# Streaming 512 instead of 256 weight columns per matmul in the projections with stationary activations

## The chip, the core and the metric

One core of a Trainium2 chip runs the whole kernel. The metric is the time on the device in microseconds, from the first to the last instruction and what the runtime has around them. Each run is one launch. In the profile TensorE's work has two rows: PE, the matmuls, and PEld, the loads of the stationary operand. VectorE is DVE, ScalarE is ACT, GpSimd is POOL, and SyncE, which issues the weight DMAs, is SP.

## The reference

An encoder trunk of two layers on 256 tokens of width 1024, in float32. Every sub-layer is pre-norm (root mean square) and residual:

```
x = x + 0.5 * swiglu(norm(x))     # up and gate 1024 -> 2816 each, down 2816 -> 1024
x = x + mixer(norm(x))
x = x + 0.5 * swiglu(norm(x))
```

Layer 0's mixer is a gated linear attention with 4 heads, in both directions: q and k of 512 columns, v and an output gate g of 1024 columns, a low-rank gate for the log decay, then a norm by head, times silu(g), and an output projection 1024 -> 1024. Layer 1's mixer is differential attention with 8 heads: q, k and v of 1024 columns each, q and k normalized over 64 columns, two softmaxes per head with a relative-position bias, p1 - lambda * p2 times v, a norm by head, and an output projection.

## The kernel before

**Precision.** A product in float32 is made of three passes in float32r, a format that TensorE takes in one pass. Every weight piece and every activation is split into a high and a low part, and the kernel adds high x high, high x low and low x high. ScalarE makes the high part of weights (a copy), VectorE the low part (a subtraction), both at line 157 of the kernel before.

**Weights.** `weight_plan` lists all weights in the order of use, in pieces of 1024 rows x 256 columns (1 MB). `prefetch` issues one DMA per piece on SP's queue, up to five pieces ahead, into 3 staging buffers. `parts` splits a piece in operations of 128 x 1024 elements, up to three pieces ahead, into 5 buffers of split weights. `next_weights` hands out the next piece and starts both for later ones. `state["hold"]` keeps splits back around the end of a sub-layer, so that the norm's operations aren't queued behind them, and `release` lets them go.

**Two forms of projection.** In the feed-forward networks, in q and k of the gated attention and in the output projections the weights are stationary and the activations are streamed: `mm3` (lines 181 and 182) streams the high and low parts of all 256 tokens, 512 columns, against the high weights and then 256 columns against the low ones; `mm1` (lines 174 to 176) makes three matmuls of 256 columns. In the projections whose result must lie with tokens on the partitions the activations are stationary, 128 tokens at a time, and the weights are streamed: `project_tok` (lines 196 to 198), for v and g of the gated attention and q, k and v of the differential one, and `down_out` (lines 388 to 390), the last down projection, which writes the kernel's output. Each of these matmuls streams the 256 columns of a piece. A column group of 256 columns takes one accumulator bank, with its two halves of 128 tokens side by side.

**Accumulators.** Pool `psA` has six banks and serves the projections, scores and attention products; `psB` has two, for transposes and small sums.

**Order.** Each mixer has an order written out by hand. In it "h" is half a column group: one half of the tokens (24 matmuls) where activations are stationary. The other steps lie between the halves. For the differential mixer: b, statistics and scaling of q and k of a pair of heads (`qk_stats`); n, their transposes (`qk_norm`); s, scores and softmax of a head; f, transposed probabilities (`flip`); a, the product with v (`attend`); o, the norm and the transposed result (`normalize`). `qk_half` holds the raw q or k of a pair of heads in its bank until b has scaled it. The output projection (`out_proj`) adds up its first two column groups in parts, with the last pairs' steps between the parts. A planner then places the instructions: each engine has one queue, worked off in order, and the planner fills it in the written order, but puts an instruction that by its own estimate isn't ready behind others that are, and a tile waits until a buffer of its pool is free.

Of the kernel before, what the change touches and what calls it, by code (L numbers as in the profile page):

```python
# [18 lines left out]
P = 128  # L19
T = 256  # L20
# [9 lines left out]
CW = 256  # L30

# [20 lines left out]
DIFF_COLS = "q0 k0 q1 k1 v0 q2 k2 v1 q3 k3 v2 v3"  # L52


def weight_plan(w):
    """The weights in the order of use: [rows, columns] pieces of at most 1024 x 256, slices of rows, columns, copies."""
    plan = []

    def cols(a, start, width=CW, times=1):
        plan.append((a[:, start : start + width], KD, width, times))  # L60

    def ffn(i, j):
        gu, down = w["ffn_w_gu"][i, j], w["ffn_w_down"][i, j]
        for c in range(FF // CW):
            cols(gu, c * CW)
            cols(gu, FF + c * CW)
        for dc in range(D // CW):
            for k0 in range(0, NFB, KD):
                n = min(KD, NFB - k0)
                plan.append((down[k0 * P : (k0 + n) * P, dc * CW : (dc + 1) * CW], n, CW, 1))  # L70

    ffn(0, 0)
    gla = w["gla_w_in"][0]
    # four times side by side, to have the ranks on four groups of partitions
    cols(gla, gla.shape[1] - 32, 32, 4)
    for kind, c in GLA_COLS.split():
        cols(gla, {"q": 0, "k": 512, "v": 1024, "g": 2048}[kind] + int(c) * CW)
# [4 lines left out]
    for kind, c in DIFF_COLS.split():  # L82
        cols(w["diff_w_in"][0], "qkv".index(kind) * D + int(c) * CW)
# [7 lines left out]
def trunk(ctx: ExitStack, tc: tile.TileContext, ins, out):  # L91
# [19 lines left out]
    def prefetch(n):  # L111
        while state["dma"] < min(len(plan), n + LOOK_DMA + 1):
            i = state["dma"]
            src, nk, width, _ = plan[i]
            t = stage.tile([P, KD, CW], F32, tag="stage", name=f"stage{i}")
            step = nk if i > 1 else 2
            for k0 in range(0, nk, step):
                ks = slice(k0, k0 + step)
                nc.sync.dma_start(t[:, ks, :width], src.rearrange("(k p) n -> p k n", p=P)[:, ks])
# [3 lines left out]
    def parts():  # L123
        """The parts of the next weights to split."""
# [3 lines left out]
        w = split[i] = wpool.tile([P, KD, 2, CW], FR, tag="w", name=f"w{i}")  # L128
        state["split"] += 1
        step = 2 if i < 2 else 4  # L130
        for k0 in range(0, nk, step):
            ks = slice(k0, min(k0 + step, nk))
            whole, wh, wl = t[:, ks, :width], w[:, ks, 0, : times * width], w[:, ks, 1, : times * width]
# [17 lines left out]
    def issue(ops, after):  # L151
        """Each operation behind those of `after` that run on its engine."""
# [6 lines left out]
    def release(*after):  # L159
        """The parts held back, behind `after`."""  # L160
# [11 lines left out]
    def mm1(ps, w, ms, act, k, first, last):  # L172
        """ps += wh.xh + wh.xl + wl.xh for one 128-deep slice."""
# [4 lines left out]
    def mm3(ps, w, ms, act, k, first, last, wk=None):  # L178
        """ps[:, 0:256] += wh.xh + wl.xh, ps[:, 256:512] += wh.xl for one 128-deep slice."""
# [11 lines left out]
    def project_tok(w, act, name, ps=None, halves=(0, 1)):  # L191
        ps = psA.tile([P, 2, CW], F32, tag="A", name=name) if ps is None else ps
        for t in halves:
            ts_ = slice(t * P, (t + 1) * P)
            for k in range(KD):
                mm(ps[:, t, :], lhsT=act[:, k, 0, ts_], rhs=w[:, k, 0, :], start=k == 0, stop=False)  # L196
# [773 lines left out]
```

## Time and profile before

| | |
|---|---|
| three runs | 1000.81, 1001.91, 1004.33 us (median 1001.91) |
| profiled execution, span (the profile lists no other time for it) | 1000.1 us |
| TensorE matmuls | 6524, busy 994.5 us (99%) |
| TensorE weight loads | 6524, busy 906.6 us (91%) |
| VectorE, ScalarE | busy 748.0 us (75%), 567.7 us (57%) |
| HBM traffic | 178.95 MB, 179 GB/s on average |

The profile's first part has each engine's busy time. Matmuls are pipelined: a matmul's shown duration overlaps the next one's, so that the time between the starts of two tells what one costs in a row of them. In time the kernel is: feed-forward (0 to 195 us), gated attention with its output projection (195 to 320), two feed-forward networks (to 690), differential mixer (to 807), and the last feed-forward network, whose down projection runs from 932 us to the end.

### The profile page before, as it was taken

Reading aid. Unit: us, or ns where it says so; the run is one execution under the profiler, and the core shown is the slowest. Engines: PE = TensorE matmul, PEld = TensorE weight load, DVE = VectorE, ACT = ScalarE, POOL = GpSimd, SP = SyncE. Lnnn points to the kernel's source line nnn. Section 1 sums busy time; section 2 is a strip of 40 time slices with the busy share of each in tenths; the row PEclk is TensorE's granted clock in tenths of the full one; section 3 lists DMA queues with packets and bytes.
Section 4 is the critical chain, followed back from the end, with each engine's and each line's share of the span. In section 5 each row is a group of like instructions: output and inputs, shape, how many; then the busy total and the mean of one; then the engine's idle time right before and its main releaser. Section 6 shows DMA issues by size and latency. Waiting matters only on the chain.

```text
span 1000.1 us, 16172 instructions
## 1 busy us (share of the span) xinstructions
PE 994.5 (99%) x6524; PEld 906.6 (91%) x6524; DVE 748.0 (75%) x1284; ACT 567.7 (57%) x962; POOL 2.0 (0%) x10
## 2 busy tenths in 40 slices
PE   9999999999999999999999999999999999999998
PEld 8888888999999888888888888889999998888998
DVE  6998756499877987774679787656989699767640
ACT  7666535397756755643456555435576577555430
POOL 0000000000000000000000000000000000000000
PEclk9999999999999999999999999999999999999999
DMA  9676544574322775545557555375655268555440
GB/s 295 221 263 209 190 158 135 194 226 154 127 85 85 256 248 178 190 159 187 167 176 248 195 184 178 128 240 171 194 149 169 65 200 274 178 171 193 158 132 22
DMA packets 176968, 178.95 MB, mean 179 GB/s; under 512 B 4419, under 2 KB 176222, under 8 KB 176894
## 3 DMA queue, kind: packets, MB, share of 16 engines
q1 hardware_dynamic: 176606, 177.68, 54.3%
q8 instruction: 51, 0.84, 0.3%
q10 hardware_dynamic: 256, 0.21, 0.1%
q14 instruction: 23, 0.19, 0.1%
q0 software_dynamic: 32, 0.02, 0.0%
HBM read 176.84 MB, written 1.06 MB: 178 GB/s over the span
## 4 chain that ended last, share of the span: by engine, by line
PE 98%; DVE 1%; DMA 0%; ACT 0%; issue 0%; ACTq 0%; POOLq 0%
PE ps_g L181 16%; PE ps_u L181 16%; PE ps_d L181 12%; PE ps_g L182 8%; PE ps_u L182 8%; PE ps_d L182 6%; PE ps_d L388 2%; PE ps_d L389 2%; PE ps_d L390 2%; PE ps_s L567 2%; PE ps_dqk L196 2%; PE ps_dqk L198 2%; PE ps_dqk L197 2%; PE ps_w L174 1%; PE ps_w L176 1%; PE ps_w L175 1%
## 5 line engine op out<-in xcount | busy, mean ns | idle before, releaser
L157 DVE TENSOR_TENSOR w<-stage,w 128x1024 fp32r<-128x1024 f32 x334 | 385.4, 1191 | 32.2 <-ACT w L157 31.9
L157 ACT ACTIVATE w<-stage 128x1024 fp32r<-128x1024 f32 x334 | 327.3, 1030 | 45.4 <-PE ps_d L390 17.0
L181 PE MATMUL ps_g<-x,w 128*128 128x512 f32 x704 | 249.3, 397 | 0.0
L181 PE MATMUL ps_u<-x,w 128*128 128x512 f32 x704 | 248.7, 395 | 0.0
L182 PE MATMUL ps_u<-x,w 128*128 128x256 f32 x704 | 197.5, 281 | 0.0
L182 PE MATMUL ps_g<-x,w 128*128 128x256 f32 x704 | 197.1, 281 | 0.0
L181 PE MATMUL ps_d<-a,w 128*128 128x512 f32 x528 | 183.2, 390 | 0.0
L181 PEld LDWEIGHTS ps_g<-x,w 128*128 128x128 f32 x704 | 132.0, 188 | 31.0 <-issue 0.9
L181 PEld LDWEIGHTS ps_u<-x,w 128*128 128x128 f32 x704 | 132.0, 188 | 30.7
L182 PE MATMUL ps_d<-a,w 128*128 128x256 f32 x528 | 149.0, 282 | 0.0
L182 PEld LDWEIGHTS ps_g<-x,w 128*128 128x128 f32 x704 | 133.4, 189 | 0.5
L182 PEld LDWEIGHTS ps_u<-x,w 128*128 128x128 f32 x704 | 133.1, 189 | 0.1
L181 PEld LDWEIGHTS ps_d<-a,w 128*128 128x128 f32 x528 | 99.1, 188 | 20.7
L182 PEld LDWEIGHTS ps_d<-a,w 128*128 128x128 f32 x528 | 99.9, 189 | 0.0
L276 ACT ACTIVATE x<-x,par 128x256 fp32r<-128x256 f32 x40 | 20.0, 507 | 117.5 <-DVE x L325 117.5
L205 ACT COPY half<-ps_u 128x256 f32<-128x256 f32 x88 | 32.7, 371 | 87.2 <-PE ps_u L182 85.4
L205 ACT COPY half<-ps_g 128x256 f32<-128x256 f32 x88 | 32.3, 370 | 83.5 <-PE ps_g L182 81.4
L206 DVE TENSOR_TENSOR up<-ps_u,half 128x256 f32<-128x256 f32 x88 | 36.9, 422 | 38.7 <-ACT half L205 38.6
L206 DVE TENSOR_TENSOR gate<-ps_g,half 128x256 f32<-128x256 f32 x88 | 36.8, 422 | 36.9 <-ACT half L205 36.9
L325 DVE SCALAR_TENSOR_TENSOR x<-ps_d,x 128x256 f32<-128x256 f32 x48 | 20.3, 424 | 57.9 <-PE ps_d L182 56.7
L388 PE MATMUL ps_d<-w,a 128*128 128x256 f32 x176 | 49.5, 281 | 0.0
L389 PE MATMUL ps_d<-w,a 128*128 128x256 f32 x176 | 49.5, 281 | 0.0
(232 smaller groups left out, 1560.6 us busy)
## 6 DMA issues: line engine op xcount, KB each, us to landing
stage<-in_ffn_w_gu_dram SPq DMA_DIRECT2D x86, 1024.0 KB, 5.1
stage<-in_ffn_w_down_dram SPq DMA_DIRECT2D x32, 1024.0 KB, 4.8
stage<-in_ffn_w_down_dram SPq DMA_DIRECT2D x16, 768.0 KB, 4.1
stage<-in_gla_w_in_dram SPq DMA_DIRECT2D x12, 1024.0 KB, 5.6
stage<-in_diff_w_in_dram SPq DMA_DIRECT2D x12, 1024.0 KB, 5.5
stage<-in_gla_w_out_dram SPq DMA_DIRECT2D x4, 1024.0 KB
stage<-in_diff_w_out_dram SPq DMA_DIRECT2D x4, 1024.0 KB, 4.9
stage<-in_ffn_w_gu_dram SPq DMA_DIRECT2D x8, 256.0 KB, 5.7
```

What stands on the lines that cost most here:

```text
L157: op()
L181: mm(ps, lhsT=w[:, wk, 0, ms], rhs=act[:, k, :, :], start=first, stop=False)
L182: mm(ps[:, 0:T], lhsT=w[:, wk, 1, ms], rhs=act[:, k, 0, :], start=False, stop=last)
L196: mm(ps[:, t, :], lhsT=act[:, k, 0, ts_], rhs=w[:, k, 0, :], start=k == 0, stop=False)
L197: mm(ps[:, t, :], lhsT=act[:, k, 0, ts_], rhs=w[:, k, 1, :], start=False, stop=False)
L198: mm(ps[:, t, :], lhsT=act[:, k, 1, ts_], rhs=w[:, k, 0, :], start=False, stop=k == KD - 1)
L205: nc.scalar.copy(h[:, b, :], ps[:, T:512])
L206: nc.vector.tensor_tensor(out=out_t[:, b, :], in0=ps[:, 0:T], in1=h[:, b, :], op=ALU.add)
L325: nc.vector.scalar_tensor_tensor(out=x[:, d, :], in0=ps[:, h * T : (h + 1) * T], scalar=coef, in1=x[:, d, :], op0=ALU.mult, op1=ALU.add,)
L388: mm(ps, lhsT=act[:, k0 + k, 0, ts_], rhs=w[:, k, 0, :], start=first, stop=False)
L389: mm(ps, lhsT=act[:, k0 + k, 0, ts_], rhs=w[:, k, 1, :], start=False, stop=False)
L390: mm(ps, lhsT=act[:, k0 + k, 1, ts_], rhs=w[:, k, 0, :], start=False, stop=last)
```

## The change

- Weights of the five projections with stationary activations come in pieces of 512 rows x 512 columns (still 1 MB); two pieces make a column group of 512 columns, the last down projection takes 6 pieces for each of two groups. The splits have two rows' slices of 512 columns, still 128 x 1024 elements.
- Each matmul streams 512 columns. A bank holds 128 tokens x 512 columns, so a column group takes two banks, one after the other.
- In the mixers a column group is done in four quarters (class `Wide`): tokens 0 to 127 with the upper 512 rows, then the lower ones, then tokens 128 to 255 likewise. "h" is now a quarter where activations are stationary (12 matmuls of 512 columns); there are 24 "h" in each mixer as before.
- In the differential mixer a group of q or k covers two pairs of heads: the groups come as q0 k0 q1 k1 v0 v1 instead of q0 k0 q1 k1 v0 q2 k2 v1 q3 k3 v2 v3. Squares, sums and scaling run on one half of the tokens and 256 columns at a time, so there are twice as many, half as long. The order is written anew. In the output projection the parts are 4, 2 and 2 slices instead of 3, 3 and 2, and the norm and transposes of pair 2 lie between them as well.
- The tiles of the first softmax have 3 buffers instead of 4; those of v are twice as large.
- In the last down projection each bank is added to x in two operations of 256 columns and stored with one DMA of 256 KB.

```diff
 ORDER = """
-h h h h h h b0 h h n0 b1 h h s00 s01 n1 h h h f0 h s10 a0 s11 h h f1 b2 n2 h o0 a1 s20 s21 h h h b3 h f2 h n3 o1 a2 s30 s31 h h o2 hold
+h h h h h h h h b0 h n0 b1 h s00 s01 n1 h h f0 h s10 s11 h h h b2 f1 h n2 b3 h s20 s21 h n3 h a0 f2 s30 s31 a1 h o0 h o1 h h a2 hold
 """
-GLA_COLS = "q0 k0 q1 k1 v1 v0 g0 g1 v2 v3 g2 g3"
+GLA_COLS = "q0 k0 q1 k1 v0 g0 v1 g1"
-DIFF_COLS = "q0 k0 q1 k1 v0 q2 k2 v1 q3 k3 v2 v3"
+DIFF_COLS = "q0 k0 q1 k1 v0 v1"
...
+    def wide(a, c, nk=KD):
+        for k0 in range(0, nk, WK):
+            n = min(WK, nk - k0)
+            plan.append((a[k0 * P : (k0 + n) * P, c * WW : (c + 1) * WW], n, WW, 1))
...
-        step = 2 if i < 2 else 4
+        step = 2 if i < 2 or width == WW else 4
...
+    def mm_tok(ps, w, act, t, k0, nk):
+        ts_ = slice(t * P, (t + 1) * P)
+        for wk in range(w.shape[1]):
+            k = k0 + wk
+            mm(ps, lhsT=act[:, k, 0, ts_], rhs=w[:, wk, 0, :], start=k == 0, stop=False)
+            mm(ps, lhsT=act[:, k, 0, ts_], rhs=w[:, wk, 1, :], start=False, stop=False)
+            mm(ps, lhsT=act[:, k, 1, ts_], rhs=w[:, wk, 0, :], start=False, stop=k == nk - 1)
+
+    class Wide:
+        def __init__(self, act, name, done):
+            self.act, self.name, self.done = act, name, done
+            self.w = []
+
+        def quarter(self, n):
+            t, kh = divmod(n, 2)
+            if t == 0:
+                self.w.append(next_weights())
+            if kh == 0:
+                self.ps = psA.tile([P, WW], F32, tag="A", name=f"{self.name}_{t}")
+            mm_tok(self.ps, self.w[kh], self.act, t, kh * WK, KD)
+            if kh == 1:
+                self.done(t, self.ps)
...
+        for c in range(D // WW):
+            banks = [psA.tile([P, WW], F32, tag="A", name=f"ps_d{c}_{t}") for t in range(2)]
+            for k0 in range(0, nk, WK):
+                w = next_weights()
+                for t, ps in enumerate(banks):
+                    mm_tok(ps, w, act, t, k0, nk)
...
+                    for b in range(2):
+                        hp = 2 * c + b
+                        if i == 0 and t == 0:
+                            tot[hp] = small.tile([P, 2, 2, 4], F32, tag="dtot", name=f"dtot{hp}")
+                        sq = d2.tile([P, CW], F32, tag="dsq", name="dsq", bufs=1)
+                        nc.scalar.activation(sq, pq[:, b * CW : (b + 1) * CW], AF.Square)
+                        nc.vector.tensor_reduce(out=tot[hp][:, i, t], in_=sq.rearrange("p (g d) -> p g d", d=64), axis=AX.X, op=ALU.add)
...
-            out_proj(o2, n2, [range(0, 3), range(3, 6), range(6, 8)], [lambda: flip(3), lambda: attend(3), lambda: release(*normalize(3))])
+            out_proj(o2, n2, [range(0, 4), range(4, 6), range(6, 8)], [lambda: (normalize(2), flip(3)), lambda: attend(3), lambda: release(*normalize(3))])
```

## Rows read from the trace of the kernel before

**Rows 1.** Page, busy time of each engine: us, share of the span, instructions.
```profile
span 1000.1 us, 16172 instructions
PE 994.5 (99%) x6524; PEld 906.6 (91%) x6524; DVE 748.0 (75%) x1284; ACT 567.7 (57%) x962; POOL 2.0 (0%) x10
```
**Rows 2.** Page, the chain of work that ended last, shares by engine.
```profile
PE 98%; DVE 1%; DMA 0%; ACT 0%; issue 0%; ACTq 0%; POOLq 0%
```
**Rows 3.** Windows: length, busy PE PEld DVE ACT POOL, clock, DMA share, GB/s.
```profile
206.00:295.00 89.00, 89.00 (x733) 88.12 (x732) 79.45 (x102) 66.00 (x122) 0.00 (x0) 1.00 0.48 154
693.00:795.00 102.00, 101.19 (x883) 99.08 (x883) 87.17 (x288) 67.31 (x161) 0.00 (x0) 1.00 0.49 154
```
**Rows 4.** Groups by line and shape, TensorE: count, busy us, mean ns, idle before.
```profile
L388 PE MATMUL ps_d<-w,a 128*128 128x256 f32 x176 | 49.5, 281 | 0.0
...
L196 PE MATMUL ps_dqk<-w,x 128*128 128x256 f32 x128 | 36.6, 286 | 0.0
...
L196 PE MATMUL ps_g<-w,x 128*128 128x256 f32 x64 | 18.8, 293 | 0.0
```
**Rows 5.** Order of time, TensorE, q and k projection: start us, duration; 11 starts.
```profile
711.74 0.28 PE L198 MATMUL ps_dqk<-w,x 128*128 128x256 f32 x1
...
712.94 0.28 PE L196 MATMUL ps_dqk<-w,x 128*128 128x256 f32 x1
```
**Rows 6.** Order of time, TensorE, last down projection; 16 starts.
```profile
994.84 0.28 PE L390 MATMUL ps_d<-w,a 128*128 128x256 f32 x1
...
996.61 0.28 PE L390 MATMUL ps_d<-w,a 128*128 128x256 f32 x1
```
**Rows 7.** Order of time, TensorE, two feed-forward networks; three pairs each.
```profile
599.70 0.39 PE L181 MATMUL ps_g<-x,w 128*128 128x512 f32 x1
...
600.74 0.39 PE L181 MATMUL ps_g<-x,w 128*128 128x512 f32 x1
...
349.73 0.40 PE L181 MATMUL ps_u<-x,w 128*128 128x512 f32 x1
...
350.79 0.40 PE L181 MATMUL ps_u<-x,w 128*128 128x512 f32 x1
```
**Rows 8.** Chain of waits, gate logits: start us, us, what.
```profile
202.41 0.92 PE ps_z L543 x4
```
**Rows 9.** Chain of waits, gated attention's products with v; eight such rows.
```profile
269.85 0.43 PE ps_av L635 x2
```
**Rows 10.** VectorE in order of time, then groups by line, VectorE and ScalarE.
```profile
706.68 0.36 DVE L792 TENSOR_SCALAR dtot<-dtot,evx 128x8 f32<-128x8 f32 x2
...
709.17 0.17 DVE L217 SCALAR_TENSOR_TENSOR dr_y<-dr_t,dr_y 128x16 f32<-128x16 f32 x1
...
L780 DVE TENSOR_REDUCE dtot<-dsq 128x8 f32<-128x512 f32 x8 | 5.5, 682 | 3.2 <-ACT dsq L779 3.2
...
L288 ACT ACTIVATE sq<-x 128x256 f32<-128x256 f32 x42 | 16.8, 404 | 0.2 <-DVE acc L289 0.2
...
L779 ACT ACTIVATE dsq<-ps_dqk 128x512 f32<-128x512 f32 x8 | 4.7, 591 | 6.5 <-PE ps_dqk L198 6.5
...
L157 DVE TENSOR_TENSOR w<-stage,w 128x1024 fp32r<-128x1024 f32 x334 | 385.4, 1191 | 32.2 <-ACT w L157 31.9
```
**Rows 11.** TensorE in order of time, tail of the differential mixer.
```profile
787.30 0.36 PE L174 MATMUL ps_w<-do,w 128*128 128x256 f32 x1
...
791.47 0.28 PE L176 MATMUL ps_w<-do,w 128*128 128x256 f32 x1
792.46 0.63 PE L891 MATMUL ps_doT<-cst,do 128*128 128x128 f32 x4 [0.71 <-DVE do L883]
```
**Rows 12.** The end, VectorE; then DMA issues with KB and median us to landing.
```profile
996.93 0.42 DVE L392 SCALAR_TENSOR_TENSOR xt<-ps_d,xt 128x256 f32<-128x256 f32 x1 [1.70 <-PE ps_d L390]
...
stage<-in_diff_w_in_dram SPq DMA_DIRECT2D x12, 1024.0 KB, 5.5
...
out_dram<-xt SPq DMA_DIRECT2D x8, 128.0 KB, 1.9
```

More of the change, by code (lines that the diff above doesn't have):

```diff
@@ L66, in ffn @@
             cols(gu, FF + c * CW)
+        if (i, j) == (1, 1):
+            for c in range(D // WW):
+                wide(down, c, NFB)
+            return
         for dc in range(D // CW):
@@ L127, in parts @@
         t = staged.pop(i)
-        w = split[i] = wpool.tile([P, KD, 2, CW], FR, tag="w", name=f"w{i}")
+        w = split[i] = wpool.tile([P, nk, 2, times * width], FR, tag="w", name=f"w{i}")
         state["split"] += 1
-        step = 2 if i < 2 else 4
+        step = 2 if i < 2 or width == WW else 4
         for k0 in range(0, nk, step):
             ks = slice(k0, min(k0 + step, nk))
-            whole, wh, wl = t[:, ks, :width], w[:, ks, 0, : times * width], w[:, ks, 1, : times * width]
+            whole, wh, wl = t[:, ks, :], w[:, ks, 0, :], w[:, ks, 1, :]
             if times > 1:
@@ L189, in project @@
         return banks
[L191 to L196, printed above, removed]
-                mm(ps[:, t, :], lhsT=act[:, k, 0, ts_], rhs=w[:, k, 1, :], start=False, stop=False)
-                mm(ps[:, t, :], lhsT=act[:, k, 1, ts_], rhs=w[:, k, 0, :], start=False, stop=k == KD - 1)
-        return ps
+    def mm_tok(ps, w, act, t, k0, nk):
[18 more added lines that the diff above has]
+                self.done(t, self.ps)
     def join(banks, out_t):
@@ L509, in project_half, with done @@
                 def project_half(kind, c, n):
+                    if kind in "vg":
+                        def done(t, ps):
+                            if kind not in tm:
+                                tm[kind] = gp.tile([P, 2, GH * DV], F32, tag=kind, name=f"{kind}_tm")
+                            nc.scalar.activation(tm[kind][:, t, c * WW : (c + 1) * WW], ps, AF.Copy, scale=norm.r[:, t : t + 1])
+                        if n == 0:
+                            half[kind, c] = Wide(norm.x2, f"ps_{kind}{c}", done)
+                        half[kind, c].quarter(n)
+                        return
                     if n == 0:
@@ L513, in project_half @@
                     w, ps = half[kind, c]
-                    if kind in "vg":
-                        project_tok(w, norm.x2, None, ps, (n,))
-                        if n == 1:
-                            if kind not in tm:
-                                tm[kind] = gp.tile([P, 2, GH * DV], F32, tag=kind, name=f"{kind}_tm")
-                            for t in range(2):
-                                nc.scalar.activation(tm[kind][:, t, c * CW : (c + 1) * CW], ps[:, t, :], AF.Copy, scale=norm.r[:, t : t + 1])
-                        return
                     for k in range(KD):
@@ L661, in raw_scores @@
                     nc.scalar.copy(sd[hp], scores(qk[:, 0, gs], qk[:, 1, gs], f"ps_s0_{hp}"))
-                halves = [partial(project_half, g[0], int(g[1]), n) for g in GLA_COLS.split() for n in range(2)]
+                halves = [partial(project_half, g[0], int(g[1]), n) for g in GLA_COLS.split() for n in range(2 if g[0] in "qk" else 4)]
                 head, tail = (o.split() for o in GLA_ORDER.split("|"))
@@ L902, in diff @@
             for kind, c in DIFF_COLS.split():
-                half_of = partial(v_half, int(c)) if kind == "v" else partial(qk_half, int(c), "qk".index(kind))
-                halves += [partial(half_of, t) for t in range(2)]
+                c = int(c)
+                group = Wide(norm.x2, f"ps_d{kind}{c}", v_done(c) if kind == "v" else qk_done(c, "qk".index(kind)))
+                halves += [partial(group.quarter, n) for n in range(4)]
             steps = {"b": qk_stats, "n": qk_norm, "s": softmax, "f": flip, "a": attend, "o": normalize}
```

79 lines of the change are left out of this document (33 added, 46 removed).

## The prediction

> **What bounds the kernel now.** I read the busy shares first, then the chain of waits, then the stages' windows, and last the single matmuls in order of time. The first two say one thing: TensorE is busy 994.5 of 1000.1 us, and 98% of the chain that ended last runs through it [rows 1, 2]. So a matmul that gets cheaper shortens the kernel directly, and everything on the other engines costs something only where it makes TensorE wait. The windows show where that could happen. In the gated linear attention (206 to 295 us) TensorE is busy without a gap and VectorE 79.45 of 89 us; in the differential mixer (693 to 795 us) TensorE has 0.8 us of gaps and VectorE is busy 87.17 of 102 us [rows 3]. So the first has a little room, and the second hardly any. The granted clock is 1.00 in both, the 2.4 GHz level.
>
> **What a matmul costs.** A matmul's shown duration (281 ns for 256 columns) overlaps the next one's, so it is no price; the step from one start to the next is. In the differential mixer's projections 10 steps take 712.94 - 711.74 = 1.20 us: 120 ns for each 256-column matmul [rows 5]. In the last down projection 15 steps take 996.61 - 994.84 = 1.77 us: 118 ns [rows 6]. 256 columns at one a cycle of 2.4 GHz are 106.7 ns, so each carries some 11 to 13 ns that don't depend on its doing more work, if that part is fixed. Whether it is fixed decides the case. The projections in the feed-forward networks run 512 and 256 columns in turn, and three such pairs take 1.04 us in one network and 1.06 us in another: 347 and 353 ns a pair [rows 7], where three 256-column steps would be 360. With 118 to 120 ns for the 256-column half, the 512-column one takes 227 to 235 ns. One place of the trace has 512-column matmuls in a row, and in just the new form (stationary activations, float32r weights streamed): the gate's logits, four in 0.92 us, 230 ns each [rows 8]. I take 230 ns, that nearest row; the ends are 227 and 236.
>
> **The sum, part by part.** *Mixers.* The old projections are three lines (196 to 198) with 128 matmuls each for q and k of the differential mixer and 64 each for its v and for v and g of the gated attention (one row of 64 stands for three) [rows 4]: 3 x (128 + 3 x 64) = 960. They become 480. Each pair of 2 x 120 = 240 ns becomes 230: 480 x 10 ns = 4.8 us gained (6.2 us at 227, 1.9 at 236). q and k of the gated attention, the output projections and the gate and up projections are not touched.
>
> *Last down projection.* Three lines with 176 matmuls each [rows 4] are 528, and become 264. 2 x 118 = 236 becomes 230: 264 x 6 ns = 1.6 us gained (2.4 at 227, nothing at 236). TensorE has no gap here and the other engines are mostly idle, so all of it is on the path.
>
> *The end.* The last bank now holds 512 columns, added in two pieces of 256: one more 0.42 us VectorE operation between the last matmul and the last store [rows 12], +0.4. That store is 256 KB instead of 128: by the rows for 128 KB (1.9 us) and for 1024 KB of weights (5.5 us) another 128 KB takes 3.6 x 128 / 896 = 0.5 us [rows 12]; nothing if 2 KB rows go faster than 1 KB ones. I take +0.4, together +0.8 (0.4 to 0.9).
>
> *VectorE and ScalarE in the differential mixer.* Squares, their sums and the scaling by the norm now run on 256 columns of one token half: 16 of each where there were 8 on 512. A VectorE operation on 256 columns from the accumulators takes 0.42 us [rows 12] against 0.68 on 512 [rows 10], so 16 x (2 x 0.42 - 0.68) / 2 for each of two kinds: 2 x 8 x 0.16 = 2.6 us more. ScalarE: 8 x (2 x 0.404 - 0.591) = 1.7 us more [rows 10], less what v's copies save. Splitting the weights costs what it did: 128x1024 a time, 1191 ns [rows 10], as many times. All this lies beside TensorE, whose projections cover it; with the cover gone it is at most 2.6 us.
>
> *The order in the differential mixer.* A column group is now four quarters (t0 upper rows, t0 lower, t1 upper, t1 lower), each 12 matmuls or 2.8 us, as long as an old half. But q of pairs 0 and 1 comes whole before k, so the statistics of pair 0 start behind quarter 8 and not behind half 4, and four of the six banks stay taken until both pairs are scaled. What TensorE can run meanwhile are quarters 9 to 12, in the last two banks: 4 x 2.8 = 11 us, and about 3.4 us of transposes and scores. VectorE must do in that time: two sums 0.8; the statistics of pair 0, 709.34 - 706.68 = 2.7 us to the end of the reciprocal root, and four scalings of 0.42, together 4.4 [rows 10]; the same for pair 1, 4.4; the normalized q and k, two operations of 0.7; one weight piece of two splits, 2.4; the four passes over the first scores, 1.4. That is 14.8 us, and 17.2 with a second weight piece, behind 0.8 us of squares: 15.6 to 18.0 against 14.4 of cover. So a gap of 1.2 to 3.6 us can open, less what the weights split ahead (three pieces) let VectorE put off. At the second pair of groups the cover is longer, since v's quarters give their banks back at once and eight of them follow. I take +1.5 (0 to 4), the old 0.8 us of gaps standing as they are.
>
> *The tail of that mixer.* The output projection's first part is now four slices long, its second two, so behind the last attention product 24 matmuls are left and not 36. Today 36 run from 787.3 to 791.5 us and TensorE then waits until 792.46 us for the scaled product [rows 11]; at (791.47 - 787.30) / 35 = 119 ns a step, 12 fewer make that wait 1.4 us longer. But the third column group's weights are split by then and one bank is free, so its matmuls can fill in. I take nothing (up to 1.4).
>
> *Weights.* Pieces are still 1 MB, in the same number. The first two quarters of a group each take a piece, the next two none: two pieces in 2.8 us, then 8.3 us without. Five buffers hold two in use and three ahead, so this costs nothing; a piece that came late would show as a wait of ScalarE for the stage.
>
> Sum for the profiled execution: 1000.1 - 4.8 - 1.6 + 0.8 + 1.5 = 996.0 us, 4.1 less. The three runs before are 1000.81 to 1004.33 us, median 1001.91, so 1.8 us above the span; the median after is forecast at 997.8 us.
>
> **A rule against this size.** Where a pass has 512 cycles (two-pass float32 on 256 columns, the attention's products with v), the step is 0.43 / 2 = 0.215 us, though each loads other weights [rows 9]: 213.3 ns of streaming and almost nothing besides. The Trainium skill says the same of any matmul (TensorE: Matmul & The Clock Gate, Back-to-back issue gap): warm, the gap is N / 2.4 plus about 2.5 ns, so 109 ns for 256 and 216 for 512 columns. For the 256-column float32r matmuls the trace doesn't agree (118 to 120), and by the rule taken whole the change would be worth 744 x 2.5 ns = 1.9 us.
>
> **Rivals.** (a) *The extra goes away at 512*: it is there because a load and a stream of 256 columns are about as long, and a longer stream hides the load. Then the new matmul takes the 215 ns of [rows 9]: 480 x 25 + 264 x 21 ns = 17.5 us gained, less 2.3: 1001.9 - 15.2 = 986.7 us. For it: those rows. Against it: the 512-column matmuls of [rows 7] and [rows 8], which also hide their loads and take 227 to 235. (b) *The extra grows with the columns*: two 120 ns make 240, or the 236 that the slower network's share suggests. Gain 0 to 1.9 us, against 2.3 of costs: 1002.3 us, no change that can be told. For it: 230 is nearly twice 118. Against it: 347 ns a pair instead of 360. (c) *The banks decide*, and the kernel gets slower. The place is the differential mixer behind quarter 8: four of six banks are held, VectorE (already busy 85% of that stage) gets 2.6 us more, and TensorE runs out of work that has a bank. At the upper count, 3.6 us there, as much again behind quarter 16, the 2.6 us uncovered, and 1.4 at the tail: 11.2 us, against 6.4 gained and 0.8 at the end: 1001.9 + 5.6 = 1007.5 us. It decides once the gaps pass 5.6 us. For it: 15.6 to 18.0 us of VectorE chain in 14.4 us. Against it: the weights are split three pieces ahead, and quarters not bound to a bank can be put forward. (d) *It isn't what it says*, for instance still 960 steps of 120 ns: the matmul count would show it; I give it no chance of its own, the edit being plain.
>
> **How the numbers follow.** Forecast 0.62, (a) 0.11, (b) 0.12, (c) 0.15. The forecast's own ends: with 227 ns and no gaps 1001.9 - 8.6 + 0.4 = 993.7; with 236 and 4 us of gaps and 1.4 at the tail 1001.9 - 1.9 + 0.9 + 5.4 = 1006.3, so its likely part is 994 to 1004. The range that should hold the time 8 times in 10 reaches part of the way to (a) and to (c): 990 to 1005. What a measurement of this kernel can tell from no change is 0.3%, 3.0 us: faster is below 998.9, slower above 1004.9. The forecast's cases lie below 998.9 about seven times in ten. Faster: 0.62 x 0.72 + 0.11 = 0.56; slower: 0.15 x 0.85 + 0.02 = 0.15; same the rest, 0.29.
>
> **What would show it.** Right: 744 fewer matmuls and as many fewer loads; 512-column steps of 227 to 236 ns in the mixers and in the last down projection; the gated attention shorter by about 2 us and still without a gap (192 pairs), the last down projection by about 1.6. Wrong, by step: a step near 215 ns means (a), near 240 (b). The order's cost is TensorE's idle time between quarters 8 and 13; over 5 us there, with VectorE's scaling or a score's accumulator as what ended it, means (c). From the last matmul to the end it should take 0.8 us more.

## The result, and the profile after

The changed kernel takes 1017.19 us (median of four runs, 1012.91 to 1018.23); the kernel before, on the same chip, 1002.15 (1000.81 to 1004.33). The ratio is 1.0142, 95% interval 1.0125 to 1.0159: slower by 1.4%, where 0.4% faster was forecast. The profiled execution is the fastest of the four: span 1011.1 us against 1000.1.

First the page of the kernel after, answering to [rows 1, 2]: span, busy time of each engine, and the chain that ended last.

```profile
span 1011.1 us, 14705 instructions
...
PE 994.3 (98%) x5780; PEld 868.8 (86%) x5780; DVE 750.5 (74%) x1298; ACT 567.6 (56%) x956; POOL 2.0 (0%) x10
...
PE 71%; DVE 3%; ACT 1%; issue 0%; DVEq 0%; ACTq 0%
```

There are 744 matmuls and 744 loads fewer, as the edit says. The chain's shares add up to 75% only, since it is followed back from the end to 235 us and no further. So 71% for TensorE beside the 98% of before shows no loss by itself: narrow_diff below, which loses nothing, has 75%. What can be read is that VectorE has 3% where it had 1%, and ScalarE 1% where it had 0%. The busy time hardly fell: a busy TensorE also counts stretches at the lower clock and single matmuls whose shown duration is longer than their step.

The matmuls themselves, TensorE in order of time, with VectorE's last operation (answering to [rows 5, 6, 12]):

```profile
697.74 0.39 PE L210 MATMUL ps_dq<-w,x 128*128 128x512 f32 x1
...
700.91 0.39 PE L212 MATMUL ps_dq<-w,x 128*128 128x512 f32 x1
...
1002.72 0.40 PE L210 MATMUL ps_d<-w,a 128*128 128x512 f32 x1
...
1006.68 0.40 PE L212 MATMUL ps_d<-w,a 128*128 128x512 f32 x1
1007.12 0.76 DVE L420 SCALAR_TENSOR_TENSOR xt<-ps_d,xt 128x256 f32<-128x256 f32 x2 [0.65 <-PE ps_d L212]
```

14 steps in 3.17 us are 226 ns, 17 steps in 3.96 us are 233 ns; 230 was assumed. So the time isn't lost in the matmuls. The windows show where it is: the stretches of [rows 3] (the mixer's stage is longer now), the whole differential mixer, and a piece of it. Columns as there: length, busy PE, PEld, DVE, ACT, POOL, clock, DMA share, GB/s.

```profile
206.00:295.00 89.00, 88.85 (x556) 79.67 (x555) 80.69 (x104) 66.89 (x117) 0.00 (x0) 1.00 0.46 155
693.00:807.00 114.00, 103.80 (x606) 87.17 (x605) 89.28 (x302) 65.50 (x163) 0.00 (x0) 0.99 0.43 137
...
689.74:819.50 129.76, 119.56 (x726) 102.21 (x725) 102.93 (x331) 76.84 (x184) 0.00 (x0) 0.99 0.44 139
...
724.20:727.60 3.40, 3.40 (x19) 3.18 (x20) 3.40 (x13) 0.26 (x1) 0.00 (x0) 0.50 0.10 10
```

The whole mixer in the kernel before:

```profile
689.89:807.21 117.32, 116.51 (x1014) 114.40 (x1014) 100.83 (x317) 77.12 (x180) 0.00 (x0) 1.00 0.49 154
```

The mixer grew from 117.32 to 129.76 us, by 12.44, and TensorE's idle time in it from 0.81 to 10.20 us. VectorE's work grew by 2.1 us only. For 3.4 us the granted clock was 0.50, the 1.2 GHz level. The stages, each from its first matmul to the next stage's first:

| us | before | after | difference |
|---|---|---|---|
| start and first feed-forward network | 195.23 | 196.28 | +1.05 |
| gated attention with output projection | 124.47 | 123.24 | -1.23 |
| two feed-forward networks | 370.13 | 370.22 | +0.09 |
| differential mixer with output projection | 117.32 | 129.76 | +12.44 |
| gate and up of the last network | 127.09 | 125.82 | -1.27 |
| last down projection | 62.36 | 61.36 | -1.00 |
| last matmul's start to the end | 3.51 | 4.44 | +0.93 |

The first, third and fifth rows hold no changed instruction. They move by as much between other runs below with the same instructions there (the two feed-forward networks take 368.1 or 370.2 us, the fifth row 125.0 to 127.1), so they are left out of the account.

TensorE's waits in the mixer of the kernel after (waiter, line, what was waited for: us in total, times, longest):

```profile
PE ps_sc L845 <- ACT qkn L835: 3.2, 2, 2.3
PE ps_sc L845 <- DVE qkx L820: 2.3, 2, 1.7
PE ps_doT L914 <- DVE do L906: 2.1, 4, 0.7
PE ps_sc L845 <- DVE mx L852: 1.0, 1, 1.0
PE ps_f L828 <- DVE qkx L820: 0.7, 2, 0.3
PE ps_sc L845 <- DVE qkn L836: 0.5, 1, 0.5
PE ps_sc L845 <- ACT dv_tm L886: 0.5, 1, 0.5
```

Scores (ps_sc) wait for normalized q and k (qkn) and, where VectorE's scaling (qkx) or a score pass (mx) is named, for an accumulator bank that it frees; so does the copy of v (dv_tm). Of these 10.3 us, 3.7 are waits of scores for qkn and 3.8 for banks. Before there was one such wait, the scaled product's 0.71 us at the tail [rows 11]. The same wait after:

```profile
806.17 0.66 PE L914 MATMUL ps_doT<-cst,do 128*128 128x128 f32 x4 [0.60 <-DVE do L906]
```

Now both engines at the first pair of heads, in order of time. TensorE:

```profile
712.02 0.39 PE L210 MATMUL ps_dq<-w,x 128*128 128x512 f32 x1
...
716.78 0.39 PE L210 MATMUL ps_dq<-w,x 128*128 128x512 f32 x1
717.51 0.30 PE L828 MATMUL ps_f<-cst,qkx 128*128 128x128 f32 x1 [0.34 <-DVE qkx L820]
...
719.91 0.38 PE L845 MATMUL ps_sc<-qkn 64*128 64x256 f32 x1 [0.87 <-ACT qkn L835]
720.80 0.85 PE L845 MATMUL ps_sc<-qkn 64*128 64x256 f32 x5 [0.52 <-DVE qkn L836]
722.61 0.98 PE L845 MATMUL ps_sc<-qkn 64*128 64x256 f32 x6 [0.95 <-DVE mx L852]
724.16 2.04 PE L845 MATMUL ps_sc<-qkn 64*128 64x256 f32 x12 [0.58 <-DVE qkx L820]
...
727.68 0.48 PE L210 MATMUL ps_dq<-w,x 128*128 128x512 f32 x1
```

and VectorE:

```profile
712.64 0.42 DVE L801 TENSOR_REDUCE dtot<-dsq 128x4 f32<-128x256 f32 x1 [1.91 <-ACT dsq L800]
...
715.81 1.22 DVE L171 TENSOR_TENSOR w<-stage,w 128x1024 fp32r<-128x1024 f32 x1
716.95 0.75 DVE L820 TENSOR_TENSOR qkx<-ps_dq,dr_y 128x256 f32<-128x256 f32 x2
717.61 0.75 DVE L820 TENSOR_TENSOR qkx<-ps_dk,dr_y 128x256 f32<-128x256 f32 x2
718.27 1.22 DVE L171 TENSOR_TENSOR w<-stage,w 128x1024 fp32r<-128x1024 f32 x1
719.41 0.68 DVE L833 TENSOR_TENSOR qkn<-ps_f,qkn 128x512 fp32r<-128x512 f32 x1
720.01 0.74 DVE L836 SCALAR_TENSOR_TENSOR qkn<-ps_f,gqk,qkn 128x512 fp32r<-128x512 f32 x1
...
722.56 1.22 DVE L171 TENSOR_TENSOR w<-stage,w 128x1024 fp32r<-128x1024 f32 x1
723.69 0.75 DVE L820 TENSOR_TENSOR qkx<-ps_dq,dr_y 128x256 f32<-128x256 f32 x2
724.36 0.74 DVE L820 TENSOR_TENSOR qkx<-ps_dk,dr_y 128x256 f32<-128x256 f32 x2
```

From quarter 8's end TensorE has two quarters to run (712.0 to 717.0 us). The next quarter, 11, whose weights are those of quarter 9, starts at 727.68: in TensorE's queue it stands behind the transposes and scores of heads 0 and 1, and these wait for VectorE's chain, which takes 12.46 us from the first sum (712.64) to the last scaling of pair 1 (725.10). Three weight splits of 1.22 us lie inside it. The same pattern comes back at pairs 2 and 3, at 748 to 770 us.

### The profile page after: what moved, and what is told of

It is laid out like the page before. It is cut to its first block, busy times and chain, and to the rows that moved or that the text cites. A ratio compares the mean times of both kernels' runs of the same rounds, so it can differ in the third digit from the quotient of the medians.

```text
span 1011.1 us, 14705 instructions
## 1 busy us (share of the span) xinstructions
PE 994.3 (98%) x5780; PEld 868.8 (86%) x5780; DVE 750.5 (74%) x1298; ACT 567.6 (56%) x956; POOL 2.0 (0%) x10
## 4 chain that ended last, share of the span: by engine, by line
PE 71%; DVE 3%; ACT 1%; issue 0%; DVEq 0%; ACTq 0%
PE ps_u L195 12%; PE ps_g L195 12%; PE ps_d L195 8%; PE ps_g L196 6%; PE ps_u L196 6%; PE ps_d L196 4%; PE ps_d L212 2%; PE ps_d L210 2%; PE ps_d L211 2%; PE ps_s L597 1%; PE ps_w L188 1%; PE ps_w L189 1%; PE ps_w L190 1%; ACT s L860 1%; PE ps_sc L845 1%; PE ps_dk L211 1%
## 5 line engine op out<-in xcount | busy, mean ns | idle before, releaser
L171 ACT ACTIVATE w<-stage 128x1024 fp32r<-128x1024 f32 x332 | 326.9, 1036 | 55.6 <-PE ps_d L212 15.3
L211 PE MATMUL ps_d<-w,a 128*128 128x512 f32 x88 | 34.8, 396 | 0.0
L212 PE MATMUL ps_d<-w,a 128*128 128x512 f32 x88 | 34.8, 395 | 0.0
```

Of the source, the lines that this page charges most:

```text
L171: op()
L211: mm(ps, lhsT=act[:, k, 0, ts_], rhs=w[:, wk, 1, :], start=False, stop=False)
L212: mm(ps, lhsT=act[:, k, 1, ts_], rhs=w[:, wk, 0, :], start=False, stop=k == nk - 1)
```

## The experiments

Below, *gaps* are what the steps from one matmul's start to the next exceed those of an unbroken row, where that is over 0.15 us; this includes some slow steps at the lower clock. *Idle* is stage less busy TensorE. Both are for the differential mixer, in the profiled execution. A ratio is taken to the kernel before as it ran beside that kernel on the same chip (medians 1002.15 to 1003.62 us).

| kernel | median us | ratio to before, 95% | mixer us | gaps | idle | us at 1.2 GHz in it |
|---|---|---|---|---|---|---|
| before | 1002.15 | | 117.32 | 1.3 | 0.8 | 0 |
| after | 1017.19 | 1.0142 (1.0125 to 1.0159) | 129.76 | 13.5 | 10.2 | 3.4 |
| narrow_diff | 1000.83 | 0.9978 (0.9967 to 0.9989) | 117.31 | 1.3 | 0.8 | 0 |
| two256 | 1023.96 | 1.0211 (1.0189 to 1.0232) | 136.42 | 15.2 | 10.8 | 13.7 |
| order_h | 1008.37 | 1.0051 (1.0034 to 1.0068) | 122.24 | 7.6 | 6.3 | 0 |
| pairs | 1001.77 | 0.9993 (0.9978 to 1.0007) | 117.81 | 4.5 | 2.7 | 0 |
| chain1 | 1013.45 | 1.0097 (1.0083 to 1.0111) | 128.58 | 11.2 | 5.6 | 10.2 |
| hold_split | 1006.11 | 1.0022 (1.0007 to 1.0037) | 122.06 | 7.1 | 4.7 | 0 |
| order_hold | 1008.26 | 1.0050 (1.0036 to 1.0064) | 124.93 | 9.6 | 5.9 | 3.4 |
| hold_tail | 1003.19 | 1.0001 (0.9989 to 1.0013) | 121.70 | 6.5 | 4.3 | 0 |
| narrow_end | 1001.14 | 0.9979 (0.9968 to 0.9990) | 117.34 | 1.3 | 0.8 | 0 |
| pairs2 | 1000.60 | 0.9978 (0.9965 to 0.9990) | 118.09 | 4.7 | 3.0 | 0 |
| pairs3 | 1001.35 | 0.9982 (0.9972 to 0.9992) | 119.34 | 5.9 | 3.6 | 0 |
| chain_long | 1004.47 | 1.0011 (1.0000 to 1.0023) | 120.87 | 4.4 | 3.3 | 0 |
| long_one | 1012.72 | 1.0099 (1.0069 to 1.0129) | 128.72 | 11.1 | 8.9 | 10.2 |
| long_all | 1018.52 | 1.0152 (1.0128 to 1.0176) | 136.10 | 15.3 | 11.4 | 13.7 |

**narrow_diff**: the old differential mixer, all else changed.

```diff
-DIFF_COLS = "q0 k0 q1 k1 v0 v1"
+DIFF_COLS = "q0 k0 q1 k1 v0 q2 k2 v1 q3 k3 v2 v3"
-        wide(w["diff_w_in"][0], ...)
+        cols(w["diff_w_in"][0], ...)
```

> The changed kernel with the differential mixer of before (256 columns a matmul, its old order and output-projection parts); the gated attention's v and g and the last down projection stay at 512. Theory 'the whole loss is in the differential mixer, the other two places gain what the shorter stream gives': 192 pairs x 9 ns + 264 x 5 ns = 3.0 us less than before, less 0.5 us at the end: 999.7 us, TensorE's gaps in that mixer as before, 1.3 us, clock 1.00. Rival 'the wide weight pieces themselves cost (weights arrive in twos, longer last store)': over 1003 us, with gaps outside the differential mixer.

The mixer is back at 117.31 us, and the kernel is 0.2% faster than before. So the whole loss is in the differential mixer, and the rest of the change is worth some 2 us.

**two256**: the new order and groups, but each 512-column matmul as two of 256.

```diff
-            mm_tok(self.ps, self.w[kh], self.act, t, kh * WK, KD)
+            for j in range(2):
+                mm_half(self.ps[:, kh * CW : (kh + 1) * CW], self.w[j], ...)
```

> The changed kernel with every 512-column matmul issued as two of 256 columns (a quarter is then one half of the columns over all eight slices, so that each accumulation closes before the next opens; four banks instead of two per group in the last down projection); order, pieces, banks of the mixers and small operations as changed. Theory 'the fixed part of a matmul is saved': 480 x 9 + 264 x 5 = 5.6 us more than the changed kernel where TensorE does not wait; in the differential mixer the longer quarters cover part of the gaps, so 3 to 6 us more in time. Rival 'a 512-column matmul costs what two of 256 do': the same time within 1 us.

Idle is 10.8 us here too. So it comes with the grouping and its order, not with the width of a matmul. The median is 6.8 us above the changed kernel's, more than the 3 to 6 expected; 13.7 us at 1.2 GHz instead of 3.4 are in the profiled mixer. What the width alone is worth shows where TensorE never waits: the last down projection takes 62.36 us here, as in the kernel before, against 61.36.

**order_h**: the changed kernel with one more quarter ahead of the first transposes and of the first scores.

```diff
-h h h h h h h h b0 h n0 b1 h s00 s01 n1 h h f0 h s10 s11 ...
+h h h h h h h h b0 h h n0 b1 h h s00 s01 n1 h h f0 s10 s11 ...
```

> The changed kernel with another written order in the differential mixer alone: both quarters of the next group stand ahead of the transposes and the next two ahead of the scores (h x8, b0 h h n0 b1 h h s00 s01 n1 h h f0 s10 s11 h h b2 f1 h h n2 b3 h h s20 s21 n3 a0 h h f2 s30 s31 a1 h o0 h o1 a2). Theory 'order': TensorE's queue is worked off in order and stands at scores whose inputs the statistics chain on VectorE has not made, with ready quarters queued behind them; with the quarters ahead the gaps around the first two and the fifth to eighth scores (9 of 13.5 us) fall to 2 or 3 us and the kernel takes 1005 us. Rival 'banks': all six banks are then held by raw q and k when the first scores come, they wait until both pairs are scaled, the gaps stay at 9 us or more and the time within 3 us of the changed kernel's.

TensorE's waits in its mixer:

```profile
PE ps_w L188 <- ACT do L916: 2.4, 1, 2.4
PE ps_sc L845 <- DVE qkx L820: 2.2, 1, 2.2
PE ps_doT L914 <- DVE do L906: 1.3, 2, 0.7
PE ps_sc L845 <- DVE mx L852: 0.3, 1, 0.3
```

Gaps fall by 5.9 us and the mixer by 7.5. No score waits for qkn any more. What stays at the scores is 2.2 us for a bank: with four quarters run ahead, all six banks are held until the scaling. So two more quarters ahead of the scores give back 7.5 of the 12.4 us. A wait for a bank is left, and another (2.4 us) at the output projection, ahead of which the order now has no quarter left. The median, 1008.37 us, stays above the 1005 expected.

**pairs**: 512 columns made of 256 of q and 256 of k of one pair of heads, v's first group 512 wide and the other two 256, in the old order. A pair's statistics then need one group only.

```diff
-DIFF_COLS = "q0 k0 q1 k1 v0 v1"
+DIFF_COLS = "p0 p1 w0 p2 p3 v2 v3"
+                plan.append(([rows[:, i * D + c * CW : i * D + (c + 1) * CW] for i in range(2)], WK, WW, 1))
```

> 512 columns a matmul, but a group of the differential mixer holds 256 columns of q and the same 256 of k, so that it serves one pair of heads as before: two banks held per pair, squares, sums and scaling on 512 columns in as many operations as before, and the old written order. v of the first two pairs is 512 wide, v of the last two stays at 256. Both theories, order and banks, expect the gaps back at before's 1.3 to 3 us and the gain of the stream kept: (192 + 192 + 48) x 9 + 264 x 5 = 5.2 us, less 0.5 at the end: 997.5 us. If instead the doubled width itself disturbs the mixer (bursts of weights), gaps over 5 us and 1003 us or more.

Gaps of 4.5 us, no wait at a score: with 512-column matmuls the mixer costs what it did. But both theories expected gaps of 1.3 to 3 us and 997.5 us, and both missed: what the stream saves (20 quarters instead of halves) goes into new gaps, at the transposes above all (1.3 us of waits, none before).

**chain1**: the changed kernel with one Newton step instead of three in the reciprocal root of q's and k's statistics.

```diff
-                r = rsqrt(tot[hp]..., [P, 16], "dr")...
+                r = rsqrt(tot[hp]..., [P, 16], "dr", 1)...
```

> The changed kernel with one Newton step instead of three in the reciprocal root of the statistics of q and k in the differential mixer; two of three steps are left out, six small VectorE operations for each pair of heads. Theory A (VectorE's chain of statistics, splits, scaling and norm sets TensorE's gaps in that mixer): the chain of each pair of heads gets about 1.2 us shorter, so the gaps fall from 13.5 to 10 to 11.5 us and the span from 1011.1 to about 1008.5. Rival B (the order in TensorE's queue alone, with gaps of fixed length): gaps 13 to 13.5 us, span 1011. Rival C (accumulator banks alone): no change either, since the same tiles are held by the same instructions in front.

Its TensorE at pair 0, the waits ahead of the first drop of the clock:

```profile
717.02 0.30 PE L828 MATMUL ps_f<-cst,qkx 128*128 128x128 f32 x1 [0.16 <-DVE qkx L820]
...
720.36 0.86 PE L845 MATMUL ps_sc<-qkn 64*128 64x256 f32 x5 [0.32 <-DVE qkn L836]
722.17 0.97 PE L845 MATMUL ps_sc<-qkn 64*128 64x256 f32 x6 [0.95 <-DVE mx L852]
```

Up to there the idle time is 1.43 us against 2.68 in the changed kernel, and VectorE's chain takes 11.20 us against 12.46: both are 1.25 us shorter. So the chain sets the wait, and rivals B and C, which let nothing change, fall. Over the whole mixer idle falls further (10.2 to 5.6 us), but part of that is TensorE working at the lower clock where it would have waited: the clock stood at 1.2 GHz for 10.2 us instead of 3.4, about 3 of the 11.2 us of gaps are 0.2 us steps at that clock, and the mixer is only 1.2 us shorter. The profiled span is 1012.0 us, where 1008.5 was expected; the medians differ by 3.7 us.

**hold_split**: the changed kernel with VectorE's weight splits issued behind the scores of heads 1 and 5.

```diff
+                elif step in ("b0", "b2"):
+                    state["hold"] = "low"
+                    qk_stats(int(step[1]))
+                elif step in ("s01", "s21"):
+                    release(softmax(int(step[1]), int(step[2])))
```

> The changed kernel with VectorE's weight splits held back from the statistics of pair 0 until the last score pass of head 1, and again from the statistics of pair 2 until that of head 5; as many splits, later. Theory A (the splits of 1.2 us each stand inside VectorE's chain): 2.4 to 4.8 us leave the chains, gaps fall from 13.5 to 9 to 10.5 us, median 1017 to about 1012. Rival B (order in TensorE's queue alone): gaps 13 to 13.5 us. Rival C (the splits are then late for the projections behind the scores): gaps unchanged in sum or larger, with weight parts named as what TensorE waits for.

Its VectorE in order of time, first sum to the last scaling of pair 1:

```profile
710.99 0.42 DVE L801 TENSOR_REDUCE dtot<-dsq 128x4 f32<-128x256 f32 x1 [1.80 <-ACT dsq L800]
...
714.28 0.75 DVE L820 TENSOR_TENSOR qkx<-ps_dq,dr_y 128x256 f32<-128x256 f32 x2
...
718.70 0.75 DVE L820 TENSOR_TENSOR qkx<-ps_dk,dr_y 128x256 f32<-128x256 f32 x2
```

719.45 - 710.99 = 8.46 us against 12.46: the splits are gone from it. Gaps fall by 6.4 us and the mixer by 7.7, more than expected, and no weight part is waited for. In the mixer this gives as much as order_h (122.06 and 122.24 us), and it takes no column, bank or matmul away. The waits for a bank go with it, but for 0.3 us. (The planner also puts pair 0's transposes five matmuls earlier and moves later scores and transposes; the same work stands ahead of the first scores.)

**order_hold**: both together.

```diff
+h h h h h h h h b0 h h n0 b1 h h s00 s01 n1 h h f0 s10 s11 ...
+                elif step in ("b0", "b2"):
+                    state["hold"] = "low"
...
```

> The changed kernel in the other written order (as in the run of the other order before), and the splits held back as well. Theory A: gaps in the mixer fall from 7.6 to 4 to 5.5 us, span 1002.6 to about 1000. Rival C (splits late): gaps 7.6 us or more, with weight parts as what is waited for. Rival D (the rest of the gaps are bank waits that no split touches): 7 to 7.6 us.

No sum of both: 124.93 us. TensorE now waits 2.5 us for qkn ahead of the transposed probabilities (ps_T) and 1.5 for a score pass, and the clock falls for 3.4 us. The planner puts TensorE's work in another order for it, so this run doesn't tell which of its rivals holds.

**hold_tail**: hold_split with the output projection's old parts.

```diff
-[range(0, 4), range(4, 6), range(6, 8)]
+[range(0, 3), range(3, 6), range(6, 8)]
```

> The changed kernel with the splits held back as before, and the output projection of the differential mixer in the old parts of 3, 3 and 2 slices instead of 4, 2 and 2, so that 36 and not 24 matmuls stand behind the last attention product. Theory (the new parts cost at the tail what was bounded at 1.4 us): of the gaps at the three scaled products behind 780 us (0.85, 0.16 and 0.73 us) some 1.0 us goes, the stage falls from 122.1 to 121.1 us. Rival (the wait for the last scaled product is there with either, as in the kernel before with 0.7 us, and the other parts only move it): stage 122 us.

0.36 us in the mixer; the waits for the scaled product stay (1.3 us, two). The rival holds: the parts don't set the tail. The new order also leaves two pairs' norms for the tail where the old one leaves one; that wasn't tried by itself. The ratio falls by 0.0021, more than 0.36 us explain; the two intervals overlap. The median is that of the kernel before, but the new groups still cost: the mixer takes 4.4 us more than before, and the 2 us that narrow_diff gains in the other places stand against it.

**narrow_end**: narrow_diff with two stores for the last bank, on two queues.

```diff
-                        nc.sync.dma_start(out[0, ts_, cs], xt[:, t, cs])
+                            (nc.sync if h else nc.scalar).dma_start(out[0, ts_, ho], xt[:, t, ho])
```

> The kernel with the old differential mixer and everything else changed, and with each 128 x 256 piece of the last bank stored by a DMA of its own, on two queues, right behind its addition. Theory (the wider bank's end costs 0.9 us through one more addition and a larger store): the end from the last matmul falls from 4.44 to 3.9 us, span 998.5 to 998.0, ratio to the kernel before 0.997. Rival (the store's fixed latency decides): end 4.4 us, span 998.5.

The end falls from 4.44 to 4.05 us, as the theory has it to 0.15 us; in the median nothing of it can be seen.

**pairs2, pairs3**: attempts at a version that beats both, from pairs with narrow_end's stores; pairs2 with n0 and n2 a quarter later, pairs3 with hold_split's hold.

```diff
-h h h h h h b0 h h n0 b1 h h s00 ... f1 b2 n2 h o0 ...
+h h h h h h b0 h h h n0 b1 h s00 ... b2 f1 h n2 o0 ...
```

> The kernel whose 512 columns are q and k of one pair of heads, with the transposes of pairs 0 and 1 put one quarter later and each 128 x 256 piece of the last bank stored on its own. Theory A (the 4.5 us of gaps of that kernel are waits for a chain that is a fraction of a quarter late): gaps 4.5 to 2.5 to 3.5 us, stage 117.8 to about 116.5, end 4.9 to 4.1 us, ratio to the kernel before about 0.997. Rival B (the gap goes to the next step in the queue): stage 117.5 to 118.5 us, ratio 0.999.

> The kernel whose 512 columns are q and k of one pair of heads, in its old order, with VectorE's splits held back from the statistics of pair 0 to the last score pass of head 1 and from those of pair 2 to that of head 5, and each 128 x 256 piece of the last bank stored on its own. Theory A (a split of 1.2 us stands inside VectorE's chain at the two transposes that wait): gaps 4.5 to 2.5 to 3.5 us, stage about 116.5 us, ratio 0.997. Rival B (there is cover here, and later splits make the projections behind the scores wait): gaps 4.5 us or more with weight parts as what is waited for, ratio 1.000.

In both the gaps don't fall (4.7 and 5.9 us), as rival B has it; its reason in pairs3, weight parts that come late, isn't among TensorE's waits. At 0.2% faster than before they are no better than narrow_diff. No version here passes that: narrow_diff, narrow_end, pairs2 and pairs3 lie within each other's intervals.

**chain_long, long_one, long_all**: narrow_diff, so old order and 256 columns, with VectorE's chain made longer by more Newton steps: 13 at pair 0, 25 at pair 0, 11 at every pair.

```diff
-r = rsqrt(tot[hp]..., [P, 16], "dr")
+r = rsqrt(tot[hp]..., [P, 16], "dr", 13 if hp == 0 else 3)
```

> The kernel with the old differential mixer and everything else changed, with 13 Newton steps instead of 3 in the reciprocal root of pair 0 alone: 30 small VectorE operations, about 0.2 us each with the way from one to the next, so the chain of pair 0 is 6 us longer; nothing else differs. Theory A (the old order has cover behind the statistics, the new one has not): less than the 6 us shows, gaps in the mixer 1.3 to between 2 and 6 us, all before the first scores. Theory C (the level of 1.2 GHz comes behind gaps): where they reach some 3 us, a stretch of 3.4 us or more at granted clock 0.5 follows in the records, and costs half its length. Rival D (the level comes with the new order's mix of scores and transposes, not with gaps): granted clock 1.00 in the mixer whatever the gaps.

> The kernel with the old differential mixer and everything else changed, with 25 Newton steps instead of 3 in the reciprocal root of pair 0 alone. Ten steps more gave 5.2 us more of VectorE and 3.1 us more of gaps, so 22 more give 11.5 us of VectorE and gaps of 4.4 + 6.3 = about 10.5 us in the mixer, one of them some 8 us long; the stage is then about 127 us. Theory C (the level of 1.2 GHz follows gaps): granted clock 0.5 for one or two stretches of 3.4 us or more right behind the long gap, and run clocks of 0.993 to 0.998. Rival D (it comes with the new order's mix of scores and transposes): granted clock 1.00 in the mixer, run clocks 0.998 to 1.000.

> The same kernel with 11 Newton steps instead of 3 for every pair of heads: some 4.2 us more of VectorE for each of four pairs, 17 us in all. Expected gaps: 1 to 3 us at each of the pairs, 6 to 12 us in all, VectorE busy nearly the whole stage; stage 122 to 130 us. Theory C (gaps): where two or more gaps lie within some 10 us of each other, a stretch at granted clock 0.5 follows, run clocks below 0.998. Theory C' (only one long gap does it, not several short ones): granted clock 1.00 here and 0.5 in the run with one long gap. Rival D: granted clock 1.00 in both.

chain_long: VectorE has 5.2 us more, the gaps grow by 3.1. The old order, then, has some 2 us of cover left at pair 0, and no drop of the clock follows a gap of 1.7 us. long_one, windows about the long gap:

```profile
709.90:715.60 5.70, 5.70 (x50) 5.70 (x48) 5.29 (x39) 2.49 (x3) 0.00 (x0) 1.00 0.01 3
715.60:719.80 4.20, 0.24 (x3) 0.03 (x1) 3.55 (x23) 0.84 (x2) 0.00 (x0) 1.00 0.00 0
719.80:730.00 10.20, 6.06 (x36) 5.17 (x37) 10.06 (x22) 1.75 (x3) 0.00 (x0) 0.50 0.33 104
730.00:740.00 10.00, 10.00 (x87) 10.00 (x86) 9.18 (x28) 9.17 (x24) 0.00 (x0) 1.00 0.80 243
```

TensorE runs unbroken, waits 6.8 us (715.8 to 722.6), and the clock stands at 0.50 from 719.8 to 730.0. In long_all, with gaps up to 2.6 us, it falls three times, for 13.7 us in all. The first fall:

```profile
727.20:734.30 7.10, 7.10 (x60) 6.95 (x58) 5.45 (x38) 6.43 (x19) 0.00 (x0) 1.00 0.28 75
734.30:736.50 2.20, 0.05 (x1) 0.03 (x1) 2.20 (x6) 0.00 (x0) 0.00 (x0) 1.00 0.01 4
736.50:737.90 1.40, 1.40 (x12) 1.38 (x13) 1.40 (x2) 0.68 (x2) 0.00 (x0) 1.00 0.00 0
737.90:741.30 3.40, 3.40 (x18) 3.40 (x17) 3.40 (x7) 0.55 (x1) 0.00 (x0) 0.50 0.56 170
```

Both runs have the old order: the level follows TensorE's gaps, and the rival that puts it down to the new mix of scores and transposes falls (D). So does the one that asks for one long gap (C'). Two or more gaps near one another (theory C) aren't needed either: one gap of 2.2 us stands ahead of the fall shown, and one of 1.8 us ahead of the second (765.2 us). Gaps of that length alone don't do it each time: order_h's two (2.2 and 2.4 us of idle time) left the clock at 1.00.

## Why the prediction was wrong

- *What a matmul costs*: right. 226 and 233 ns, between the ends 227 and 236 but for 1 ns. Neither 215 (rival a) nor 240 (rival b) came. The 216 ns that the prediction quotes from the Trainium skill (TensorE: Matmul & The Clock Gate, Back-to-back issue gap) are given there for a matmul by itself, without its load; no 512-column float32r step measured here is that short.
- *Mixers, stream*: 1.23 us in the gated attention where 192 pairs x 10 ns = 1.9 were expected. A quarter takes 2.86 us against an old half's 2.955, so 16 quarters give 1.5 us; a new 0.3 us gap takes the rest. For the differential mixer's 24 quarters that is 2.3 us instead of 2.9.
- *Last down projection and the end*: -1.00 and +0.93 us, where -1.6 and +0.8 were expected; they cancel.
- *VectorE and ScalarE*: 2.1 us more VectorE in the mixer (expected 2.6); its size was right, its cover wasn't.
- *The order in the differential mixer*: **the step that failed.** It reads "What TensorE can run meanwhile are quarters 9 to 12, in the last two banks: 4 x 2.8 = 11 us", and takes +1.5 us (0 to 4). Measured: gaps +12.2 us. The chain was not longer than reckoned: 12.46 us from the first sum to the release of pair 1's banks (15.6 to 18.0 were reckoned, with work that comes behind that). The cover was half: the written order is b0 h n0 b1 h s00 s01 n1 h h, so only quarters 9 and 10 stand ahead of the first scores. 11 and 12 stand behind them in a queue that is worked off in order, though their weights had been used for 9 and 10, and 11 starts at 727.68 us. The sixth bank, which the prediction gave to them, goes to the scores of head 0. Counting free banks told what TensorE *could* run; the order tells what it *does* run. order_h, which moves two quarters ahead, and hold_split, which takes 4.0 us out of the chain, each give back 7.5 to 7.7 of the 12.4 us.
- *That the second pair of groups has longer cover*: wrong for the same reason. At 748 to 770 us gaps of 0.5, 0.7, 1.8 and 2.5 us open.
- *The weights split ahead*: they were said to let VectorE put splits off. It doesn't unless told: each stands in VectorE's queue where the plan put it, three of them inside the chain.
- *The tail*: taken as nothing, up to 1.4. That was right for the wait that it speaks of, the one ahead of the last scaled product: 0.60 us against 0.71 before. The 2.1 us of such waits are four; the other three stand at the products of the earlier pairs, which had none before, and with the old parts two are left (hold_tail).
- *Not foreseen*: the clock. A stretch of 3.4 us at 1.2 GHz costs about half of itself, 1.7 us, in the profiled execution: in it pair 1's eight transposes take 1.54 us to the start of the next matmul, in hold_split at clock 1.00 they take 0.85. The other three runs had mean clocks of 0.989 to 0.995 against its 0.998 and spans 3.5 to 5.3 us longer; long_one's four had 0.990 to 0.995, while hold_split, with 4.7 us of idle time instead of 10.2, had 0.998 to 1.000 and the kernel before 0.996 to 1.000. That fits the distance of the median from the profiled time, but these runs have no trace that shows where the clock fell.

The account of the profiled mixer: +12.2 gaps, -2.3 stream, +1.7 clock (partly inside the gaps) = 11.6 of 12.4 us; some 0.8 us, in the longer first steps behind each break, is not put down to single instructions. Rival (c) had the side and the place (behind quarter 8 and behind 16) but 7.2 us instead of the 9.7 measured there. Its mechanism, banks, is the smaller part: 3.8 of the 10.3 us of waits in the kernel after, 2.2 in order_h. Most of it hangs on the late chain too, since hold_split, with the same banks and order, has 0.3 us of it left.

The Trainium skill warns that short idle times between groups of matmuls let the clock go back and forth (TensorE: Matmul & The Clock Gate, A second HAM failure mode: psum-queue depth-cycling). The trace agrees: no idle time ahead of the drop at 724.2 us was longer than 0.95 us.

## What to carry to other kernels

Count the cover of a wait in the order of the engine's own queue, from the waiting instruction backwards: work that is ready but stands behind it covers nothing. Where a product of several column groups has to be complete before a chain may start, make the wide group out of the columns that the chain needs together (q and k of one pair), and put work that can wait, such as weight splits, behind that chain in its engine's queue. And give TensorE's gaps a price above their length, since the clock may fall behind them.

## What the runs showed of the hardware

- A lower clock followed gaps of TensorE of very different length: five idle times of at most 0.95 us (after), one of 1.2 us (chain1, second drop), one of 1.8 or 2.2 us (long_all), one of 6.8 us (long_one). Single ones of 1.6 us (chain_long), 2.2 and 2.4 us (order_h) and 2.3 us (after, at 769.8 us) did without. So the length of a gap doesn't decide it alone; what else does stays open. The stretches last 3.4, 6.8 or 10.2 us. It can eat most of a cut in the chain: chain1's mixer had 4.6 us less idle and 6.8 us more at the low level, and was 1.2 us shorter.
- The same instructions of the two middle feed-forward networks take 368.1 us in some profiled executions and 370.2 in others, at clock 1.00 in both; [rows 7] has both steps, 347 and 353 ns a pair. What selects them stays open.
- A store of 256 KB as two of 128 KB on two queues shortens the end by 0.4 us (4.44 to 4.05).
